# Gates and branch projections with tokens on partitions, merged rows turned by VectorE and DRAM

## The chip, the cores and the metric

The kernel runs on one core of a Trainium2 chip. A core has a matrix engine (TensorE, PE in the profile; its weight loads are PEld), a vector engine (VectorE, DVE), a scalar engine (ScalarE, ACT), a general engine (GpSimd, POOL) and a queue engine that issues transfers (SyncE, SP). They run side by side and wait for each other by semaphores. Data lies in a working memory of 128 partitions (SBUF), in the matrix engine's accumulation banks (PSUM) and in DRAM. The metric is the device time of one execution in microseconds (us). Lower is better.

## The reference

The model is an encoder of two layers on 256 tokens with 1024 channels, all in float32. The part that matters here is the token mixer of each layer:

```python
def _token_mixer(xn, w_in, w_pool, pool_scale, w_a, w_b, w_o, rel_bias):
    u, q, k, v, g_pool, g_attn = jnp.split(xn @ w_in, SPLITS, axis=-1)
    ...   # pool_out (256 x 1024) from u, attn_out (256 x 512) from q, k, v
    merged = jax.nn.sigmoid(g_pool) * (pool_out @ w_a) + jax.nn.sigmoid(g_attn) * (attn_out @ w_b)
    return merged @ w_o
```

The result is added to the residual, and a normalisation, a gated MLP with a short convolution, and another residual follow. So four products stand before the merge: the pool branch (1024 x 1024), the pool gate and the attention gate (1024 x 1024 each) and the attention branch (512 x 1024). One product stands behind it: the output projection (1024 x 1024).

## The kernel before

**Numbers in two parts.** Every float32 operand of a large product is split into a high part, rounded to the matrix engine's format (fp32r), and a low part, the rest. A product is the sum of three: high x high, high x low and low x high. ACT makes the high part of a weight piece with a copy (line 191), DVE the low part with a subtraction (line 192).

**Weights.** The class `Weights` plans all loads at the start. A load is 1 MB and goes into one of three raw buffers (`RAW`); it holds two pieces of 128 x 1024 numbers. A piece is split into one of five pairs of buffers named `wh` and `wl` (`BUFS`), up to three pieces ahead of the one in use (`LOOK`); the first four pieces of the MLP go to buffers of their own that lie idle at that time. `load` issues on SP, `_split` makes the split, `get` hands a piece out, `free` gives it back. `queue_behind` takes a few instructions and a number of pieces, whose splits are then issued behind these instructions on ACT and DVE. Each engine works its instructions off in one fixed order, which a scheduler sets when the kernel is built. The SP queue, too, is worked off in order: a transfer whose buffer is not yet free holds up those behind it.

**Products with channels on partitions.** `proj` takes a piece of 128 output channels and all 1024 input channels as the stationary side, and the tokens as the moving side. `two_sums` issues, for each of the eight input chunks, one matmul of 512 columns (the high weights with the high and the low parts of the 256 tokens, side by side) and one of 256 columns (the low weights with the high parts). That is a pair per input chunk. The two sums lie in two halves of a bank, and `add_up` (lines 567 and 568) adds them: ACT copies one, DVE adds the other.

**Products with tokens on partitions.** The value projections and the start of the MLP use `v_sum`: 128 tokens are the stationary side, and 512 output channels of the weights are the moving side. Each input chunk takes three matmuls of 512 columns. The output projection (`residual_mm`, lines 573 to 575) works in this form too, since it is added to the residual, which lies by tokens. Its first four input chunks run over both token halves and both channel halves at once (48 matmuls); the last four are held and used output by output, so that the norm of the first outputs can begin.

**The order around the change.** The pool branch (`pa`, lines 1073 to 1077) runs in eight chunks of 128 channels, with steps of the attention between them. Then come eight chunks of the pool gate (`gate`, a tanh in place of the sigmoid, with the halves folded in elsewhere), which multiply `pa`. Then, twice, four chunks of the attention gate and four of the attention branch (`b_ps`): DVE multiplies and adds, and the merged chunk `m` of 128 channels is split by ACT (line 1111) and DVE (line 1112) into the two parts `mh` and `ml`, which the output projection takes as its stationary side. Channels are on partitions throughout, as the output projection wants them.

Of the kernel before, what the change touches and what calls it, by code (L numbers as in the profile page):

```python
# [16 lines left out]
P = 128  # L17
# [77 lines left out]
class Weights:  # L95
# [8 lines left out]
    def __init__(self, tc, pool, idle):  # L104
# [5 lines left out]
        self.behind, self.n_behind = (), 0  # L110
# [35 lines left out]
    def queue_behind(self, insts, n):  # L146

        self.behind, self.n_behind = insts, self.n_split + n

    def _split(self, upto):  # L150
        nc = self.nc
        first = self.n_split
        while self.n_split < len(self.pieces):
# [7 lines left out]
            with ExitStack() as queued:  # L161
                if i < self.n_behind:
                    for inst in self.behind:
                        queued.enter_context(self.tc.issue_after(inst.ins))
# [56 lines left out]
def encoder(ctx, tc, x, w_in, w_pool, pool_scale, w_a, w_b, w_o, norm1, norm2, w_up, conv_w,  # L221
# [28 lines left out]

    for l in range(DEPTH):
# [20 lines left out]
        for c in range(4):  # L272
            W.use(cols(w_a[l], c * 256))
        for c in range(4):
            W.use(cols(w_in[l], C_GP + c * 256))
        for c in range(2):
            W.use(cols(w_in[l], C_GA + c * 512))
            W.use(cols(w_in[l], C_GA + c * 512 + 256))
            src = w_b[l][:, c * 512 : (c + 1) * 512].rearrange("(k p) c -> p k c", p=P)
            W.use(  # L280
                W.add(
                    src, (4, 512),
                    [((lambda t, j=j: t[:, :, j * 256 : (j + 1) * 256]), (4, 256)) for j in (0, 1)],
                )
            )
        for c in range(4):
            W.use(rows(w_o[l], c * 256))
        slots = (("v1",), ("ybig",), ("at2",))
# [236 lines left out]
    def columns(banks, wh, wl, k0=0):  # L525


        return [
            (
                ps,  # L530
                lambda k, c=c: wh[:, k0 + k, c * P : (c + 1) * P],
                lambda k, c=c: wl[:, k0 + k, c * P : (c + 1) * P],
            )
            for c, ps in enumerate(banks)
        ]

# [20 lines left out]
    def halves(a):  # L557

        return a.rearrange("p (t m) -> p t m", t=2)
# [89 lines left out]
    def v_sum(ps, x2, t, n, piece):  # L649
# [3 lines left out]
        for m, (part, w, j) in enumerate(passes):  # L653
            nc.tensor.matmul(  # L654
                ps, x2[:, 2 * n + j, part, t, :], w[:, j, :], start=(n + m == 0),
                stop=(n == 3 and m == 5),
            )

# [178 lines left out]
    for l in range(DEPTH):  # L837
# [235 lines left out]
        pa = big.tile([P, KD, S], F32, tag="ybig", name="pa")  # L1073
        for c in range(KD):
            add_up(pa[:, c, :], proj(po2))
            if c not in (1, 6):
                step()
# [3 lines left out]
        gates = big.tile([P, 4, S], F32, tag="gates", name="gates")  # L1081

        def gate(c):
            th = gates[:, c % 4, :]
# [181 lines left out]
```

## Time and profile before

| | |
|---|---|
| time, median of 3 runs | 874.62 us (874.56 to 874.74) |
| the profiled execution's own time | 874.7 us |
| its span, first to last instruction | 872.8 us |
| PE busy | 865.6 us (99%), 4807 matmuls |
| DVE busy | 680.1 us (78%) |
| ACT busy | 526.1 us (60%) |
| POOL busy | 31.3 us (4%) |
| read from DRAM | 159.8 MB, 184 GB/s over the span |

The profile is one execution, taken by the hardware. A group line names a source line, an engine, an operation and what it writes and reads, then a count, the busy time in us and the mean ns of one, and the idle time of the engine before these instructions with what ended it. A transfer line gives the size and the median time from its issue to its landing. The chain of work that ended last is followed back from the last instruction, at each step to what released it; an engine's share of it tells what the time is made of. The lines of `proj` and `add_up` are those of a helper, so their groups are told apart by the tiles' names: `po` is the pool branch's input, `x` the normed tokens, `at` the attention's output.

### The profile page before, as it was taken

Reading aid. Unit: us, or ns where it says so; the run is one execution under the profiler, and the core shown is the slowest. Engines: PE = TensorE matmul, PEld = TensorE weight load, DVE = VectorE, ACT = ScalarE, POOL = GpSimd, SP = SyncE. Lnnn points to the kernel's source line nnn. Section 1 sums busy time; section 2 is a strip of 40 time slices with the busy share of each in tenths; the row PEclk is TensorE's granted clock in tenths of the full one; section 3 lists DMA queues with packets and bytes.
Section 4 is the critical chain, followed back from the end, with each engine's and each line's share of the span. In section 5 each row is a group of like instructions: output and inputs, shape, how many; then the busy total and the mean of one; then the engine's idle time right before and its main releaser. Section 6 shows DMA issues by size and latency. Waiting matters only on the chain.

```text
span 872.8 us, 12725 instructions
## 1 busy us (share of the span) xinstructions
PE 865.6 (99%) x4807; PEld 756.8 (87%) x4807; DVE 680.1 (78%) x1158; ACT 526.1 (60%) x927; POOL 31.3 (4%) x98
## 2 busy tenths in 40 slices
PE   9999999999999999999999999999999999999997
PEld 8888889988888888888888889999888888888886
DVE  7998786757869978878855987776678698887874
ACT  7656554556647766666545674545666486666662
POOL 1800000000000000000000000000000000000000
PEclk9999999999999999999999999999999999999999
DMA  9676545345555475465636565453556446556531
GB/s 331 234 250 201 185 149 190 128 163 193 189 173 193 153 232 193 156 228 196 240 121 219 168 219 168 146 185 105 193 180 229 158 156 223 190 174 212 193 145 49
DMA packets 125958, 161.70 MB, mean 185 GB/s; under 512 B 3320, under 2 KB 106432, under 8 KB 125896
## 3 DMA queue, kind: packets, MB, share of 16 engines
q1 hardware_dynamic: 125736, 160.62, 54.7%
q8 instruction: 38, 0.62, 0.3%
q10 hardware_dynamic: 160, 0.27, 0.1%
q14 instruction: 24, 0.20, 0.1%
HBM read 159.80 MB, written 1.07 MB: 184 GB/s over the span
## 4 chain that ended last, share of the span: by engine, by line
PE 99%; DMA 0%; ACT 0%; POOLq 0%; issue 0%; DVE 0%; SPq 0%; POOL 0%; DVEq 0%; ACTq 0%
PE proj_ps L519 61%; PE v_ps L654 6%; PE res_ps L575 6%; PE res_ps L573 6%; PE res_ps L574 6%; PE b_ps L519 3%; PE v_ps L829 3%; PE v_ps L736 1%; PE pool_ps L519 1%; PE o_ps L1020 1%; PE s_ps L970 1%; PE pt_ps L999 1%; PE s_ps L965 1%; PE o_ps L1016 1%; PE xt_ps L457 1%; DMA raw<-in_w_in_dram 0%
## 5 line engine op out<-in xcount | busy, mean ns | idle before, releaser
L192 DVE TENSOR_TENSOR wl<-raw,wh 128x1024 fp32r<-128x1024 f32 x274 | 334.0, 1223 | 108.7 <-ACT wh L191 54.4
L191 ACT CAST wh<-raw 128x1024 fp32r<-128x1024 f32 x274 | 286.2, 1049 | 84.6 <-PE proj_ps L519 36.5
L519 PE MATMUL proj_ps<-x,wh 128*128 128x512 f32 x1408 | 335.0, 390 | 0.0
L519 PEld LDWEIGHTS proj_ps<-x,wh 128*128 128x128 f32 x1408 | 260.5, 188 | 51.7
L519 PEld LDWEIGHTS proj_ps<-x,wl 128*128 128x128 f32 x1408 | 176.7, 191 | 4.2
L519 PE MATMUL proj_ps<-x,wl 128*128 128x256 f32 x1408 | 179.8, 283 | 0.0
L573 PE MATMUL res_ps<-wh,actq 128*128 128x512 f32 (+1 forms) x184 | 70.0, 380 | 0.0
L574 PE MATMUL res_ps<-wl,actq 128*128 128x512 f32 (+1 forms) x184 | 69.9, 380 | 0.0
L575 PE MATMUL res_ps<-wh,actk 128*128 128x512 f32 (+1 forms) x184 | 69.9, 380 | 0.0
L574 PEld LDWEIGHTS res_ps<-wl,actq 128*128 128x128 f32 x184 | 34.6, 188 | 6.6
L575 PEld LDWEIGHTS res_ps<-wh,actk 128*128 128x128 f32 x184 | 34.6, 188 | 6.6
L573 PEld LDWEIGHTS res_ps<-wh,actq 128*128 128x128 f32 x184 | 34.6, 188 | 6.6
L1192 ACT ACTIVATE y<-y 128x256 f32<-128x256 f32 x44 | 18.1, 416 | 28.5 <-DVE y L1183 28.4
L519 PE MATMUL proj_ps<-po,wh 128*128 128x512 f32 x128 | 32.2, 396 | 0.0
L430 POOL TENSOR_SCALAR ss<-ss 128x1 f32<-128x1 f32 x8 | 2.0, 244 | 799.4 <-ACT junk L423 799.4
L1179 ACT ACTIVATE y<-a,prm 128x256 f32<-128x256 f32 x36 | 21.6, 600 | 14.8 <-DVE a L568 14.8
L519 PEld LDWEIGHTS proj_ps<-po,wh 128*128 128x128 f32 x128 | 23.1, 189 | 4.2
L573 PE MATMUL res_ps<-wh,m 128*128 128x512 f32 (+1 forms) x72 | 26.5, 368 | 0.0
L575 PE MATMUL res_ps<-wh,m 128*128 128x512 f32 (+1 forms) x72 | 26.3, 365 | 0.0
L574 PE MATMUL res_ps<-wl,m 128*128 128x512 f32 (+1 forms) x72 | 26.3, 365 | 0.0
L567 ACT COPY gates<-proj_ps 128x256 f32<-128x256 f32 x32 | 11.9, 373 | 23.4 <-PE proj_ps L519 23.4
L423 ACT ACTIVATE junk<-h 128x512 f32<-128x512 f32 (+1 forms) x19 | 10.5, 553 | 25.5 <-DVE h L421 25.3
(209 smaller groups left out, 1130.1 us busy)
## 6 DMA issues: line engine op xcount, KB each, us to landing
raw<-in_w_in_dram SPq DMA_DIRECT2D x58, 1024.0 KB, 5.2
raw<-in_w_up_dram SPq DMA_DIRECT2D x44, 1024.0 KB, 6.4
raw<-in_w_down_dram SPq DMA_DIRECT2D x22, 1024.0 KB, 4.9
raw<-in_w_a_dram SPq DMA_DIRECT2D x8, 1024.0 KB, 5.1
raw<-in_w_o_dram SPq DMA_DIRECT2D x8, 1024.0 KB, 4.8
raw<-in_w_b_dram SPq DMA_DIRECT2D x4, 1024.0 KB, 4.8
raw<-in_w_pool_dram SPq DMA_DIRECT2D x2, 1024.0 KB, 5.0
gain<-in_norm_dram SPq DMA_DIRECT2D x3, 512.0 KB, 4.3
```

Of the source, the lines that this page charges most:

```text
L191: lambda: nc.scalar.copy(out=h, in_=src),
L192: lambda: nc.vector.tensor_sub(out=l, in0=src, in1=h.bitcast(F32)),
L423: nc.scalar.activation(junk[:, 0 : cc.stop - cc.start], h[:, t, cc], AF.Square, scale=D**-0.5, accum_out=ss[:, n : n + 1],)
L519: nc.tensor.matmul(out, w(k), x, start=(steps is first and k == 0), stop=(steps is last and k == nk - 1), skip_group_check=turns["rest"],)
L567: nc.scalar.copy(out=out, in_=sums[1])
L573: nc.tensor.matmul(ps, ah, wh, start=first, stop=False, skip_group_check=on)
L574: nc.tensor.matmul(ps, ah, wl, start=False, stop=False, skip_group_check=on)
L575: nc.tensor.matmul(ps, al, wh, start=False, stop=last, skip_group_check=on)
L654: nc.tensor.matmul(ps, x2[:, 2 * n + j, part, t, :], w[:, j, :], start=(n + m == 0), stop=(n == 3 and m == 5),)
L829: nc.tensor.matmul(ps[t], a[:, k, t, :], w[:, j, :], start=(k + m == 0), stop=(k == KD - 1 and m == 2),)
L1179: nc.scalar.activation(y, a, AF.Identity, bias=b, scale=w1)
L1192: nc.scalar.activation(y2, y, AF.Square, scale=float(np.sqrt(0.044715)))
```

## The change

The pool branch, both gates and the attention branch are computed with tokens on partitions: `by_tokens` takes two banks, one for each 128 tokens, and runs `v_sum` over pieces of 256 input channels x 512 output channels. The weights are cut accordingly (`rows` in place of `cols`). All matmuls of these products are 512 columns wide, three per input chunk, token half and channel half. `two_sums` stays for the other products; `columns` goes.

The gates' tanh reads its bank directly, and the pool branch is copied by ACT from its bank; there are no two sums to add any more. The merged rows now have tokens on partitions, but the output projection still wants channels there. So each half of 512 channels is turned: `turn_blocks` has DVE turn it in blocks of 32 x 32 numbers, and `to_chunks` writes the turned blocks to DRAM (one transfer of 512 KB), reads them back (four transfers of 128 KB, each to 32 partitions), and splits them into `mh` and `ml` with two instructions each on ACT and DVE. This happens once per half, so twice in each layer. All five transfers go through the SP queue.

`queue_behind` can now hold several entries, each with a range of pieces. In the built kernel the splits of the fourth output-projection piece stand behind the first half's last split; the low parts of the last four stand behind the last turn; and the first four pieces of the MLP stand behind the second half's last split.

```diff
--- before.py
+++ after.py
@@ -107,7 +107,7 @@
         self.n_loaded, self.n_split, self.n_got = 0, 0, 0
         self.raw, self.split = {}, {}
         self.live = set()
-        self.behind, self.n_behind = (), 0
+        self.behind, self.later = (), []
         self.n_scaled, self.gains = 0, None
 
     def add(self, src, shape, cuts, tag=None):
@@ -143,9 +143,12 @@
             self.nc.sync.dma_start(out=t[:, c : c + step], in_=src[:, c : c + step])
             yield
 
-    def queue_behind(self, insts, n):
-
-        self.behind, self.n_behind = insts, self.n_split + n
+    def queue_behind(self, insts, n, first=0):
+
+
+        first = max(first, self.n_split)
+        self.later = self.later[-2:] + [(insts, range(first, first + n))]
+        self.behind = insts
 
     def _split(self, upto):
         nc = self.nc
@@ -159,8 +162,8 @@
                 break
             self.load(n + 1)
             with ExitStack() as queued:
-                if i < self.n_behind:
-                    for inst in self.behind:
+                for insts, some in self.later:
+                    for inst in insts if i in some else ():
                         queued.enter_context(self.tc.issue_after(inst.ins))
                 for part in self.open_next():
                     for make in part[:2]:
@@ -248,6 +251,7 @@
             tag,
         )
 
+    first_up = []
     for l in range(DEPTH):
         for g in range(NG):
             c0 = C_V + g * 512
@@ -269,22 +273,15 @@
                 pool = (pool[:1], pool[1:])
             W.use(pool[0] + cols(w_in[l], C_Q + c * 256))
             W.use(pool[1] + cols(w_in[l], C_K + c * 256))
-        for c in range(4):
-            W.use(cols(w_a[l], c * 256))
-        for c in range(4):
-            W.use(cols(w_in[l], C_GP + c * 256))
-        for c in range(2):
-            W.use(cols(w_in[l], C_GA + c * 512))
-            W.use(cols(w_in[l], C_GA + c * 512 + 256))
-            src = w_b[l][:, c * 512 : (c + 1) * 512].rearrange("(k p) c -> p k c", p=P)
-            W.use(
-                W.add(
-                    src, (4, 512),
-                    [((lambda t, j=j: t[:, :, j * 256 : (j + 1) * 256]), (4, 256)) for j in (0, 1)],
-                )
-            )
+        for w, c0 in ((w_a[l], 0), (w_in[l], C_GP)):
+            for c in (c0, c0 + 512):
+                W.use(rows(w, 0, 4, c, 512) + rows(w, 512, 4, c, 512))
+        for c in (0, 512):
+            W.use(rows(w_in[l], 0, 4, C_GA + c, 512) + rows(w_in[l], 512, 4, C_GA + c, 512))
+            W.use(rows(w_b[l], 0, 4, c, 512))
         for c in range(4):
             W.use(rows(w_o[l], c * 256))
+        first_up.append(len(W.pieces))
         slots = (("v1",), ("ybig",), ("at2",))
         for j in range(2):
             W.use(rows(w_up[l], j * 512, 4, 0, 512), slots[2 * j : 2 * j + 2])
@@ -521,18 +518,6 @@
                     stop=(steps is last and k == nk - 1), skip_group_check=turns["rest"],
                 )
         turns["rest"] = not turns["rest"]
-
-    def columns(banks, wh, wl, k0=0):
-
-
-        return [
-            (
-                ps,
-                lambda k, c=c: wh[:, k0 + k, c * P : (c + 1) * P],
-                lambda k, c=c: wl[:, k0 + k, c * P : (c + 1) * P],
-            )
-            for c, ps in enumerate(banks)
-        ]
 
     ready = []
 
@@ -646,15 +631,53 @@
     def v_tile():
         return acc.tile([P, 512], F32, tag="acc", name="v_ps")
 
-    def v_sum(ps, x2, t, n, piece):
+    def v_sum(ps, x2, t, n, piece, last=3):
+
 
         _, (wh, wl) = piece
         passes = [(0, wh, 0), (0, wl, 0), (1, wh, 0), (0, wh, 1), (0, wl, 1), (1, wh, 1)]
         for m, (part, w, j) in enumerate(passes):
             nc.tensor.matmul(
                 ps, x2[:, 2 * n + j, part, t, :], w[:, j, :], start=(n + m == 0),
-                stop=(n == 3 and m == 5),
+                stop=(n == last and m == 5),
             )
+
+    def by_tokens(x2, n, at_once=1, then=None):
+
+        ps = [mmp.tile([P, 512], F32, tag="mm", name="t_ps") for _ in range(2)]
+        for i0 in range(0, n, at_once):
+            held = [W.get() for _ in range(at_once)]
+            for t in range(2):
+                for i, piece in enumerate(held, i0):
+                    v_sum(ps[t], x2, t, i, piece, n - 1)
+            for i, _ in held:
+                W.free(i)
+            if then:
+                then()
+        return ps
+
+    def turn_blocks(y, t, rows):
+
+        return nc.vector.transpose(out=y[:, :, :, t, :].rearrange("p q c j -> p c q j"), in_=rows)
+
+    def to_chunks(y, z, x2):
+
+
+
+        d = dram.tile([P, 4, 256], F32, tag="turned", bufs=2, name="turned")
+        nc.sync.dma_start(out=d, in_=y.rearrange("p q c t j -> p q (c t j)"))
+        for q in range(4):
+            src = d[:, q].rearrange("(a i) x -> i a x", a=4)
+            nc.sync.dma_start(out=z[32 * q : 32 * q + 32].rearrange("p a c t j -> p a (c t j)"), in_=src)
+        for c in range(0, 4, 2):
+            cs = slice(c, c + 2)
+            src = z[:, :, cs].rearrange("p a c t j -> p a (c t) j")
+            hi, lo = (p[:, cs].rearrange("p c t (a j) -> p a (c t) j", a=4) for p in x2)
+            last = (
+                nc.scalar.copy(out=hi, in_=src),
+                nc.vector.tensor_sub(out=lo, in0=src, in1=hi.bitcast(F32)),
+            )
+        return last
 
     def two_parts(tag, name):
 
@@ -1070,47 +1093,52 @@
                 if m >= 3 and n % 2:
                     step()
 
-        pa = big.tile([P, KD, S], F32, tag="ybig", name="pa")
-        for c in range(KD):
-            add_up(pa[:, c, :], proj(po2))
-            if c not in (1, 6):
-                step()
+
+        pa = big.tile([P, 2, D], F32, tag="ybig", name="pa")
+        places = iter(range(KD))
+        for cc in HALVES:
+            ps = by_tokens(po2, 4, then=lambda: step() if next(places) not in (1, 6) else None)
+            for t in range(2):
+                nc.scalar.copy(out=pa[:, t, cc], in_=ps[t])
         assert not steps
 
 
-        gates = big.tile([P, 4, S], F32, tag="gates", name="gates")
-
-        def gate(c):
-            th = gates[:, c % 4, :]
-            add_up(th, proj(x2, 2))
-            nc.scalar.activation(th, th, AF.Tanh, scale=0.5)
+        def gate():
+            th = big.tile([P, 2, 512], F32, tag="gates", name="gates")
+            ps = by_tokens(x2, 4)
+            for t in range(2):
+                nc.scalar.activation(th[:, t], ps[t], AF.Tanh, scale=0.5)
             return th
 
-        for c in range(KD):
-            th = gate(c)
-            nc.vector.scalar_tensor_tensor(
-                out=pa[:, c, :], in0=th, scalar=1.0, in1=pa[:, c, :], op0=ALU.add, op1=ALU.mult
-            )
+        for cc in HALVES:
+            th = gate()
+            for t in range(2):
+                nc.vector.scalar_tensor_tensor(
+                    out=pa[:, t, cc], in0=th[:, t], scalar=1.0, in1=pa[:, t, cc],
+                    op0=ALU.add, op1=ALU.mult,
+                )
         m2 = big.tile([P, 2, KD, 2, P], F32R, tag="m2", name="m2")
         mh, ml = m2[:, 0], m2[:, 1]
-        for c4 in range(2):
-            ths = [gate(4 * c4 + j) for j in range(4)]
-            for j2 in range(2):
-                i, (wh, wl) = W.get()
-                both = [mmp.tile([P, 2, S], F32, tag="mm", name="b_ps") for _ in range(2)]
-                two_sums(at2, 4, *columns(both, wh, wl))
-                for j, ps in enumerate(both):
-                    c = 4 * c4 + 2 * j2 + j
-                    m = sm.tile([P, S], F32, tag="u", name="m")
-                    add_up(m, (ps[:, 0], ps[:, 1]))
+        z = big.tile([P, 2, 4, 4, 2, 32], F32, tag="q1", name="merged")
+        for n, cc in enumerate(HALVES):
+            th = gate()
+            ps = by_tokens(at2, 2, 2)
+            y = big.tile([P, 4, 4, 2, 32], F32, tag=("q0", "k0")[n], name="turned")
+            for t in range(2):
+                with tc.issue_after(last[1].ins) if n else ExitStack():
                     nc.vector.scalar_tensor_tensor(
-                        out=m, in0=ths[2 * j2 + j], scalar=1.0, in1=m, op0=ALU.add, op1=ALU.mult
+                        out=th[:, t], in0=th[:, t], scalar=1.0, in1=ps[t], op0=ALU.add, op1=ALU.mult
                     )
-                    nc.vector.tensor_add(out=m, in0=m, in1=pa[:, c, :])
-                    m = halves(m)
-                    nc.scalar.copy(out=mh[:, c], in_=m)
-                    nc.vector.tensor_sub(out=ml[:, c], in0=m, in1=mh[:, c].bitcast(F32))
-                W.free(i)
+                    nc.vector.tensor_add(out=th[:, t], in0=th[:, t], in1=pa[:, t, cc])
+                    turned = turn_blocks(y, t, th[:, t])
+                last = (None, turned)
+            ks = slice(4 * n, 4 * n + 4)
+            last = to_chunks(y, z[:, n], (mh[:, ks], ml[:, ks]))
+            if n == 0:
+
+                W.queue_behind(last, 5, first_up[l] - 5)
+        W.queue_behind((turned,), 4, first_up[l] - 4)
+        W.queue_behind(last, 4, first_up[l])
 
         x2 = two_parts("x", "x2")
         norm = Norm(to_channels(x2, acc, g2))
```

## The prediction, made before the changed kernel was run

> **What bounds the kernel now.** I read the chain that ended last first, from the page, to see which engine a saving has to come from.
>
> ```profile
> PE 99%; DMA 0%; ACT 0%; POOLq 0%; issue 0%; DVE 0%; SPq 0%; POOL 0%; DVEq 0%; ACTq 0%
> ```
>
> TensorE (PE) is the chain, and it waits for 1.0 us in the whole span, in two places in the opening. So every nanosecond of PE work taken away is time saved, and every wait put before PE is time added: no slack elsewhere absorbs it. Next, the same chain in order of time (start, length, what), for the pitch of PE's two kinds of work:
>
> ```profile
> 174.22 33.38 PE proj_ps L519 x192
> 207.60 5.57 PE b_ps L519 x32
> ...
> 443.83 27.23 PE v_ps L654 x120
> ```
>
> The 192 matmuls of the gates are 96 pairs of one 512-wide and one 256-wide matmul: 33.38/96 = 0.3477 us a pair. The 32 of the attention branch are 16 pairs of 0.348. The 120 of the value projection are all 512 wide: 27.23/120 = 0.2269 each. This is the form that the change goes to. Then the groups by line, for the work of VectorE (DVE) and ScalarE (ACT) between the branches and the output projection:
>
> ```profile
> L192 DVE TENSOR_TENSOR wl<-raw,wh 128x1024 fp32r<-128x1024 f32 x274 | 334.0, 1223 | 108.7 <-ACT wh L191 54.4 <-PE proj_ps L519 45.7 <-issue 6.8
> L191 ACT CAST wh<-raw 128x1024 fp32r<-128x1024 f32 x274 | 286.2, 1049 | 84.6 <-PE proj_ps L519 36.5 <-PE res_ps L575 22.6 <-DMA raw<-in_w_up_dram 7.5
> L421 DVE TENSOR_TENSOR h<-res_ps,h 128x512 f32<-128x512 f32 x12 | 8.2, 687 | 6.7 <-PE res_ps L575 6.7
> L816 ACT CAST x<-xu 128x512 fp32r<-128x512 f32 x4 | 2.4, 614 | 1.6 <-DVE xu L811 1.6
> ```
>
> A weight piece costs ACT 1.05 and DVE 1.22; a 128x512 step costs DVE 0.69 and ACT 0.61. Last, the transfers (size, median us from issue to landing) and the SP queue around the one existing trip through DRAM:
>
> ```profile
> raw<-in_w_o_dram SPq DMA_DIRECT2D x8, 1024.0 KB, 4.8
> bt<-fd SPq DMA_DIRECT2D x5, 256.0 KB, 5.7
> out_dram<-xn SPq DMA_DIRECT2D x3, 256.0 KB, 2.4
> ```
>
> ```profile
> 52.06 0.37 SPq L131 DMA_DIRECT2D raw<-in_w_pool_dram  x1
> 52.52 5.00 SPq L398 DMA_DIRECT2D bt<-fd  x5
> ```
>
> See the second: a 256 KB read issued 0.46 us behind a 1 MB load needs 5.7 us to land, although 256 KB alone are stored in 2.4. Transfers of the SP queue go in order.
>
> **What the change saves on PE.** Per layer it recasts the pool branch (64 pairs), both gates (128) and the attention branch (8 chunks of 4, 32): 224 pairs x 0.3478 = 77.9 us. In their place stand 224 x 1.5 = 336 matmuls of 512 x 0.2269 = 76.2 us. Saved: 1.7 a layer, 3.4 in all. No other PE work changes. Evacuation gets cheaper (two ACT copies of 512 in place of an ACT copy and a DVE add per 256 columns), but that lay beside PE, so it is worth nothing. The new form needs a weight piece every 12 x 0.227 = 2.72 us; ACT needs 1.05 and DVE 1.22 for it, so PE keeps being fed. The loads are cut into runs of 2 KB instead of 1 KB, the same bytes; they land in 4.8 where they are rows already (w_o) and in 5.2 where not (w_in), both far inside the 5.4 us that a load's two pieces last: nothing.
>
> **What it adds: the way from the branches to the output projection.** Before, a merged chunk of channels was cast on the spot. Now each half (512 channels) is merged by DVE (multiply, add, turn, for both token halves), written to DRAM, read back by four reads, and cast. The first half has 72 matmuls = 16.3 us of PE work over it (second gate half and branch half) and needs about 15, so I cost it at nothing; what it does is keep DVE busy until just before the second half. The second half has only the output projection's first four steps over it: 48 x 0.227 = 10.9 us. I work it out with T = the moment PE starts the output projection (229.7 in layer 0 of before), by the order in which the built kernel's instructions stand on each engine.
>
> DVE's order for the second half is: multiply of token half 0, the low part of the fourth output-projection piece, add, turn, multiply of half 1, add, turn. There are five weight buffers, so this fourth piece takes that of the first piece of the last branch weight, which PE leaves six matmuls before T: T-1.4. ACT casts it to T-0.3, DVE's low part is done at T+1.0, and five steps of 0.69 with a few hundredths between them end at T+4.6 to T+4.8. A turn is in no row; its bounds are 0.49 (L987, one input, 128x512) and two passes, 1.22. I take 0.69, the copy of the same size out of PSUM (L1155, 0.68), the nearest in shape.
>
> The write (512 KB) is issued at T+4.8. Two stores of 256 KB issued 0.4 us apart land 2.4 us after the first (864.1 to 866.5): T+7.2.
>
> Between the write and the reads stands a 1 MB load of w_up on SP. It needs a raw buffer, that is, the low parts of two more pieces, which DVE makes behind the last turn: T+4.8 + 2 x 1.22 = T+7.2. It lands 4.7 to 5.0 later (least and median of all loads): T+12.1.
>
> The four reads of 128 KB are issued behind it, from T+7.6, and go in order: the bias reads ran at some 300 GB/s behind their load, so 512 KB take 1.7 us: T+13.8. Without the load in front they would need 2.4 like the stores, or 3.1 as they are issued 0.4 apart, and land by T+10.3: this is the lower end. In all SP issues twenty transfers more (0.4 each), and the write makes it wait for the turn; behind that stand w_up loads whose pieces PE wants only after the output projection, at T+22, so this costs nothing by itself.
>
> ACT waits for all four, then casts (0.61): T+14.5. PE wants this at T+10.9: a wait of 3.6. The low part follows 0.69 later, and PE wants it two matmuls on: 0.3 more.
>
> Behind it on DVE: three low parts of w_up pieces (3.7 us) stand ahead of the first residual add, and ACT's casts for them start only after the merged ones. The second add of h, which was PE-bound at 5.6 us after PE reached its fifth step, comes some 7.5 after PE resumes; the norm's row chain takes 2.5 from there, and PE's turning of the normed rows, which had about 0.6 us to spare, waits some 0.5 (0 to 1.3).
>
> Sum per layer: 3.6 + 0.3 + 0.5 = 4.4 added, 1.7 saved, 2.7 net; two layers 5.4. The profiled execution took 874.7 (span 872.8 and 1.9 around it; the median is 874.62, the same within 0.1): **880.1**.
>
> Bounds of the added part per layer: 0.8 if the reads land by T+10.3 (0.3 for the cast, 0.3, 0.2); 3.5 if they queue, with turns of 0.49 and the norm on time; 6.3 with turns of 1.22 (1.1 more) and the norm 1.3 late (0.8 more). One thing stands apart: the reads fill 32 partitions each. [...]
>
> **Rivals.**
> (1) *The return is on time*; faster. Place: the four reads. It needs them not to queue behind the w_up load, or DVE's part to end three us earlier. For it: transfers were busy only a half of the time here (DMA share 0.49 to 0.58 around 216 to 240). Against: the load is earlier in the queue, and the bias reads. It decides where the wait per layer falls under 1.7. With 0.8 a layer: 874.7 - 3.4 + 1.6 = 872.9.
> (2) *Half on time*: the load's transfer is mostly through when the reads come, the wait is 1.3 to 2.1 a layer, some 1.7: 874.7, no change.
> (3) *The clock falls in the wait.* Mechanism: a PE that stands still loses its granted clock.
>
> ```profile
> 866.70:869.10 2.40, 0.00 (x0) 0.00 (x0) 0.91 (x2) 1.20 (x3) 0.76 (x2) 1.00 0.00 0
> 869.10:872.80 3.70, 0.00 (x0) 0.00 (x0) 0.00 (x0) 0.00 (x0) 0.00 (x0) 0.50 0.38 144
> ```
>
> These stretches (PE, weight loads, DVE, ACT, POOL, granted clock) begin after PE's last matmul at 866.6: 2.5 us later the clock is at 0.50. My wait of 3.6 is longer. Against: no wait inside the kernel shows it. Price: the opening's matmuls start at 0.8 and the clock stands at full by 5.5, so at most 4.7 us at half speed, 2.4 lost; I take 1.5 a layer, of which 0.2 hide the late norm: 874.7 + 5.4 + 2.6 = 882.7. [...]
> (4) *The first half is late too*: its reads stand behind a w_o load and land some 12 us after its branch, ACT wants them at 12.8. If they are 2 us later, DVE's second half moves with them: 874.7 + 5.4 + 2 x 1.0 = 882.1.
>
> **How the numbers follow.** Chances: forecast 0.53 (878.3 to 883.9 by its own bounds of 3.5 and 6.3), clock 0.17, first half late 0.06, half on time 0.10, on time 0.14. 0.2% (1.75 us) is about what a measurement of this kernel can tell from no change. So faster 0.14, same 0.10, slower 0.76. The range reaches from rival 1 to the upper end of the forecast, which the clock's case reaches too: 872.9 to 884.0.
>
> **What the profile after would show.** PE's stretches of 48 matmuls on t_ps at 10.9 us instead of 11.1; the transpose on DVE at some 0.69; a write landing in 2.4 and reads 5 to 6 us after their issue; one wait of 3 to 4 us on PE at L558, released by the cast of L677, and a short one at L560 by L678, per layer; a short wait before the transposes of the normed rows. I am wrong if the reads land within 3.5 us of the write, if the turn costs far from 0.69, or if the clock falls.

## The result, and the profile after

The changed kernel took 887.61 us (median of 6 runs, 883.65 to 890.09) against 874.59 for the kernel before, measured beside it. The ratio is 1.0144, with a 95% interval of 1.0121 to 1.0167: slower by 1.4%. The prediction said 880.1, within 872.9 to 884.0. The direction was right, the time lies outside the range. The profiled execution took 887.53 (span 885.7), 12.8 more than the profiled one of before (span 872.8).

In the chain that ended last, shares of the span by engine, PE has fallen from 99% to 92%, and a chain of transfers and of DVE, SP and ACT steps has come into it:

```profile
PE 92%; DMA 4%; DVE 2%; SPq 1%; ACT 1%; issue 0%; POOLq 0%; POOL 0%; ACTq 0%
```

PE's waits (who waited for whom: us in total, times, longest us). Before, there was nothing on this list beyond the opening's 1.0; behind the opening there is now one entry:

```profile
PE res_ps L558 <- ACT m L677: 10.2, 2, 5.8
```

So the output projection waits once per layer for the cast of the second half of the merged rows. The same chain in order of time, layer 0 (start, length, what), shows how the return comes about:

```profile
174.01 46.29 PE t_ps L640 x204
...
221.32 4.76 DMA merged<-turned
...
226.18 0.63 ACT m L677
226.83 0.56 DVE m L678
227.44 0.68 DVE m L678
228.13 0.60 DVE gates L1129
228.72 1.14 DVE wl L195
229.86 0.61 DVE gates L1132
230.50 0.71 DVE turned L661
...
232.54 0.72 DVE turned L661
233.28 2.96 DMA turned<-turned
...
237.57 5.41 DMA merged<-turned
243.08 0.63 ACT m L677
243.75 0.80 PE res_ps L558
244.54 0.43 PE res_ps L559
```

Read it from the top. The new products have the pitch that was forecast, 46.29/204 = 0.2269 us. The lines from 221.32 to 227.44 are the first half's return: its reads, its cast and its low parts, and DVE starts on the second half only behind them. The chain in layer 1 runs the same way. PE starts the output projection at T = 228.28. DVE merges and turns until 233.25, the write takes 2.96 to land, the fourth read 5.41, and the cast lets PE go on at 243.75. PE had been ready since 239.32: a wait of 4.43, and in layer 1 one of 5.77. And then the matmuls come 0.43 apart where 0.23 is their pitch: the clock has fallen. Stretches of 3.41 us around the two waits (busy us and number of instructions of PE, weight loads, DVE, ACT and POOL, then granted clock, DMA share and GB/s), first layer 0:

```profile
239.61:243.02 3.41, 0.00 (x0) 0.00 (x0) 0.00 (x0) 0.00 (x0) 0.00 (x0) 1.00 1.09 298
243.02:246.43 3.41, 2.68 (x6) 2.11 (x7) 2.52 (x4) 3.35 (x5) 0.00 (x0) 0.50 0.64 212
246.43:249.85 3.42, 3.42 (x9) 2.64 (x8) 2.84 (x3) 1.57 (x2) 0.00 (x0) 0.50 0.25 72
249.85:253.26 3.41, 3.41 (x16) 2.82 (x15) 1.94 (x3) 0.90 (x3) 0.37 (x1) 1.00 0.89 288
```

and layer 1:

```profile
676.51:679.93 3.42, 0.00 (x0) 0.00 (x0) 0.00 (x0) 0.00 (x0) 0.00 (x0) 1.00 1.08 300
679.93:683.34 3.41, 2.03 (x5) 1.62 (x6) 1.88 (x3) 2.70 (x4) 0.00 (x0) 0.50 0.75 257
683.34:686.75 3.41, 3.41 (x10) 2.67 (x9) 2.91 (x3) 2.22 (x3) 0.00 (x0) 0.50 0.07 23
```

In each layer the clock stands at 0.50 for 6.83 us, in which PE works for 2.68 + 3.42 = 6.1 and 2.03 + 3.41 = 5.4 us. At full clock that is half as long: 3.05 + 2.7 = 5.8 us lost. With the waits of 10.2 this makes 16.0, against a gain that the third experiment measures in its profile as 3.0 (span 869.8). 16.0 - 3.0 = 13.0; the spans differ by 12.9.

### The profile page after: what moved, and what is told of

Read it like the earlier page. It is cut to its first block, busy times and chain, and to the rows that moved or that the text cites. A ratio compares the mean times of both kernels' runs of the same rounds, so it can differ in the third digit from the quotient of the medians.

```text
span 885.7 us, 12137 instructions
## 1 busy us (share of the span) xinstructions
PE 868.5 (98%) x4583; PEld 748.1 (84%) x4583; DVE 661.9 (75%) x1070; ACT 509.3 (57%) x847; POOL 31.0 (3%) x98
## 4 chain that ended last, share of the span: by engine, by line
PE 92%; DMA 4%; DVE 2%; SPq 1%; ACT 1%; issue 0%; POOLq 0%; POOL 0%; ACTq 0%
PE proj_ps L516 45%; PE t_ps L640 14%; PE v_ps L640 6%; PE res_ps L558 6%; PE res_ps L559 6%; PE res_ps L560 6%; DMA merged<-turned 2%; PE v_ps L852 2%; PE pool_ps L516 1%; PE v_ps L759 1%; DMA turned<-turned 1%; PE pt_ps L1022 1%; PE o_ps L1043 1%; PE s_ps L993 1%; PE s_ps L988 1%; PE o_ps L1039 1%
## 5 line engine op out<-in xcount | busy, mean ns | idle before, releaser
L516 PE MATMUL proj_ps<-x,wh 128*128 128x512 f32 x1152 | 274.5, 390 | 0.0
L516 PEld LDWEIGHTS proj_ps<-x,wh 128*128 128x128 f32 x1152 | 213.1, 188 | 42.2
L516 PEld LDWEIGHTS proj_ps<-x,wl 128*128 128x128 f32 x1152 | 144.9, 191 | 3.6
L516 PE MATMUL proj_ps<-x,wl 128*128 128x256 f32 x1152 | 147.9, 283 | 0.0
L640 PE MATMUL t_ps<-wh,x 128*128 128x512 f32 x256 | 79.6, 390 | 0.0
L640 PEld LDWEIGHTS t_ps<-wh,x 128*128 128x128 f32 x256 | 48.1, 188 | 10.0
L640 PE MATMUL t_ps<-wl,x 128*128 128x512 f32 x128 | 49.8, 389 | 0.0
L640 PE MATMUL t_ps<-wh,po 128*128 128x512 f32 x128 | 42.7, 399 | 0.0
L558 PE MATMUL res_ps<-wh,m 128*128 128x512 f32 (+1 forms) x72 | 29.1, 404 | 10.2 <-ACT m L677 10.2
L1207 ACT ACTIVATE y<-a,prm 128x256 f32<-128x256 f32 x36 | 21.6, 600 | 14.7 <-DVE a L553 14.7
L640 PEld LDWEIGHTS t_ps<-wl,x 128*128 128x128 f32 x128 | 24.0, 188 | 4.9
```

The source lines that it names most:

```text
L516: nc.tensor.matmul(out, w(k), x, start=(steps is first and k == 0), stop=(steps is last and k == nk - 1), skip_group_check=turns["rest"],)
L558: nc.tensor.matmul(ps, ah, wh, start=first, stop=False, skip_group_check=on)
L640: nc.tensor.matmul(ps, x2[:, 2 * n + j, part, t, :], w[:, j, :], start=(n + m == 0), stop=(n == last and m == 5),)
L1207: nc.scalar.activation(y, a, AF.Identity, bias=b, scale=w1)
```

## The experiments

The theory after the result: the time is the saving of the new form, plus PE's wait for the second half's return, plus the clock that falls in this wait. The wait is longer than forecast because of the return's own parts (the load in front of the reads, the reads' rate, the first half ahead of it). The rivals were that the clock only accompanies something else, that the load in front is all of the wait, and that the new form itself is slower. All profiled spans below are set against the 869.8 of the kernel without the trip.

### PE kept busy over the return

```diff
+        if keep:
+            keep()
         then, half = None, None
...
+            ps = mmp.tile([P, 512], F32, tag="mm", name="idle_ps")
+            for _ in range(16):
+                nc.tensor.matmul(ps, mh[:, 0, 0, :], mh[:, 0:2], start=True, stop=True)
```

> Sixteen matmuls of 512 columns whose result nobody reads (3.6 us) are put on PE in each layer between the output projection's fourth and fifth step, where PE now stands still for 4.4 us (layer 0) and 5.8 us (layer 1). Theory (the 13 us lost are 10.2 us of waiting for the second half's return, plus some 5.8 us because the halved clock then lasts 6.8 us in each layer, less 3.4 us saved on PE): the wait is used up by the idle matmuls and is no longer, the clock stays at full, 881.8 us (881 to 883). Rival (the clock record goes with the wait but costs nothing by itself): 887.6 us. Rival (PE waits for something that comes a fixed time after it gets there, not for the return): 894 us, as the idle matmuls add 7.3 us.

It took 883.76 (881.92 to 886.86), ratio 1.0109 (1.0085 to 1.0134): by the medians faster than the changed kernel by 3.9, although PE does more (the ranges of the two overlap). PE's waits:

```profile
PE res_ps L558 <- ACT m L679: 3.5, 2, 2.1
```

The stretches of 3.41 us in layer 0 and then in layer 1 (columns as above):

```profile
240.53:243.94 3.41, 2.05 (x10) 1.36 (x8) 0.06 (x1) 0.71 (x2) 0.00 (x0) 1.00 1.10 300
243.94:247.35 3.41, 3.41 (x14) 2.50 (x15) 3.23 (x4) 3.41 (x5) 0.00 (x0) 1.00 0.36 126
...
677.44:680.85 3.41, 1.65 (x6) 1.10 (x7) 1.50 (x3) 2.32 (x4) 0.00 (x0) 1.00 0.98 301
680.85:684.26 3.41, 3.41 (x10) 2.65 (x9) 3.41 (x4) 2.60 (x3) 0.00 (x0) 0.50 0.04 6
```

In layer 0 PE stood still for 1.4 us and the clock stayed. In layer 1 the return came later, PE stood still for 2.1 us, 1.76 of them inside one stretch, and the clock fell for 3.41. So the clock's loss is of its own, and it goes when PE has work; but the sixteen matmuls did not cover the whole wait. The four runs show what this leaves to chance: the two with a mean granted clock of 0.999 and 1.000, which has no room for a fall, took 881.9 and 882.7, as expected; the two with 0.998 and 0.997 took 884.8 and 886.9.

### The reads ahead of the load

```diff
+                if self.reads is not None and self.first_late <= self.n_loaded < self.first_late + 2:
+                    queued.enter_context(self.tc.issue_after(self.reads.ins))
                 self.last = self.nc.sync.dma_start(out=t, in_=src)
...
+        W.first_late = W.pieces[first_up[l]][0] + 1
```

> One transfer changes its place: the load of the second half of the first w_up rows is issued on SP behind the second half's four reads, not between the write and them. Theory (the reads are late because they queue behind that 1 MB load): they are issued about 7.5 us after PE starts the output projection and need about 3.5 us to land instead of 6 to 7, the wait falls from 4.4 and 5.8 us to 1 to 2 us, the clock has no time to fall, and the kernel takes 874 to 877 us. Rival (the trip through DRAM is slow by itself, through the write's completion and the four narrow reads): the wait falls by under 1 us a layer and the clock still falls, 884 us or more.

880.98 (878.36 to 885.73), ratio 1.0092 (1.0061 to 1.0123). Its waits, and the return in its chain in order of time:

```profile
PE res_ps L562 <- ACT m L681: 4.3, 2, 2.2
```

```profile
232.88 2.96 DMA turned<-turned
...
237.18 3.15 DMA merged<-turned
```

The read lands 3.15 behind its issue instead of 5.41, and the waits go from 10.2 to 4.3. So the load in front is about half of the wait: in layer 0, where the last turn ended at T + 4.9 for T + 5.0, the wait fell from 4.4 to 2.1. In layer 1 it fell from 5.8 to 2.2, but there the last turn also ended at T + 4.9 instead of T + 6.0, which this edit does not touch. Of the profiled run's 6.8 us over the kernel without the trip (876.6 against 869.8), 4.3 is waiting and 1.7 a fall of the clock for 3.41 us in layer 1, behind a wait of only 2.24. This is the fastest of the four runs; the three others have a mean granted clock of 0.994 or 0.995 against its 0.997, so they spent more time at half clock.

### No trip through DRAM

```diff
-        d = dram.tile([P, 4, 256], F32, tag="turned", bufs=2, name="turned")
-        nc.sync.dma_start(out=d, in_=y.rearrange("p q c t j -> p q (c t j)"))
...
-            src = z[:, :, cs].rearrange("p a c t j -> p a (c t) j")
+            src = y[:, :, cs].rearrange("p a c t j -> p a (c t) j")
```

> The write and the reads are left out; ACT and DVE split what the turn left in place, so the merged values that the output projection gets are wrongly placed and the output is not the reference's. All else is the changed kernel. Theory (PE's part of the change is worth 3.4 us and everything lost comes from the trip): no wait of PE, 874.6 - 3.4 = 871.2 us (870.8 to 872.0). Rival (the token form of the products is itself dearer than by its pitch, through weight loads, bank changes or late weight pieces): 874.6 us or more.

871.73 (871.32 to 871.84), ratio 0.9966 (0.9953 to 0.9979). PE waits in the opening only:

```profile
PE gain_ps L345 <- PEq L1271: 0.8, 1, 0.8
```

This is the other half of the change alone. The new form saves 2.8 us by the medians (874.55 - 871.73; forecast 3.4), nothing of it is late, and its five runs lie within 0.5 us, where those of the changed kernel lie within 6.4. All the loss is in the trip.

### Reads that fill all partitions

```diff
-            src = d[:, q].rearrange("(a i) x -> i a x", a=4)
-            nc.sync.dma_start(out=z[32 * q : 32 * q + 32].rearrange("p a c t j -> p a (c t j)"), in_=src)
+            nc.sync.dma_start(out=z[:, q].rearrange("p c t j -> p (c t j)"), in_=d[:, q])
```

> The four reads of each half keep their size (128 KB) and their pieces of 1 KB, but each goes to all 128 partitions instead of 32, so the values are wrongly placed and the output is not the reference's. Theory that the reads ran at half rate because of their 32 partitions: their part of the transfer falls from 2.6 us to about 1.4, the wait falls by 1.1 to 1.2 us in each layer, 885.3 us, and 882 us if the clock then keeps up in one of the layers. Rival (their pace of some 230 GB/s is that of 1 KB pieces read back from DRAM): no change, 887.6 us.

881.58 (881.39 to 883.93), ratio 1.0087 (1.0072 to 1.0102), waits:

```profile
PE res_ps L558 <- ACT m L676: 6.5, 2, 3.4
```

While the reads' data flow, in the changed kernel (32 partitions each; last columns granted clock, DMA share, GB/s):

```profile
240.50:242.50 2.00, 0.00 (x0) 0.00 (x0) 0.00 (x0) 0.00 (x0) 0.00 (x0) 1.00 1.12 256
```

and in this kernel (128 partitions):

```profile
240.00:241.50 1.50, 0.00 (x0) 0.00 (x0) 0.00 (x0) 0.00 (x0) 0.00 (x0) 1.00 1.07 374
```

The transfer engines are as busy in both, with pieces of 1 KB in both, but move 256 GB/s in the one stretch and 374 in the other. The median read lands after 4.4 instead of 6.1. The wait falls from 4.4 to 3.4 in layer 0 and from 5.8 to 3.0 in layer 1. Only the first is mostly the reads' rate: the last turn ended 0.2 us earlier there than in the changed kernel, and 2.1 us earlier in layer 1, because the first half came back sooner. The clock now falls for one stretch of 3.41 in each layer and not for two: 6.5 + 2 x 1.7 = 9.9, and the span is 879.7 - 869.8 = 9.9 longer. The time is near the 882 of the expectation by luck: that needed the clock to hold through one of the layers, and it fell in both. That reads of 32 partitions go at half the rate was the author's assumption, and no run shows it: these stretches lose a third (256 of 374). Nor does a run isolate what the partitions cost: the four narrow reads go to four different groups of 32 partitions, some pieces of the next load lie in both stretches, and the edit also changes the order in which the rows are read.

### Reads first, and PE kept busy

The edits of the first two experiments together, with ten matmuls in place of sixteen.

> As the run with the reads ahead of the load, and PE also runs ten unread 512-wide matmuls (10 x 0.227 = 2.27 us a layer) in the time of the two waits of 2.1 to 2.2 us that were left there; the output is the same. Theory (the waits and the clock are all there is): the waits go to under 0.2, the clock never falls, and the time is 874.6 - 3.4 + 2 x 2.27 = 875.7, from run to run within 1 us. Rival (something behind the return is late as well, DVE's low parts or the norm): PE waits elsewhere by 0.5 to 1.3 a layer, 877 to 878.5.

880.72 (880.43 to 883.44), ratio 1.0066 (1.0049 to 1.0083): neither expectation. The waits of the profiled run:

```profile
PE res_ps L562 <- ACT m L683: 2.3, 2, 1.8
```

The matmuls took their 2.27 us a layer, but the second half came back later than in the kernel that it builds on: its casts start 13.2 and 14.4 us behind T, there 12.5 and 12.6. What is late there is the first half. In both kernels its reads still stand behind a w_o load, its own casts start 1.5 and 1.2 us ahead of T instead of 2.2, and DVE's work on the second half is queued behind its low parts. So the cover was eaten up, and in the profiled run (883.44, span 881.6) the clock also fell twice for 3.41 us, in the opening at 6.99 and in layer 1. In the three other runs, at 880.4 to 880.9, the mean granted clock (0.999) leaves no room for a fall; where they lose what lies above the expected 875.7 is open, since the slowest run alone has a trace.

### Wide reads that reach the right places, in front of the load

```diff
-        for q in range(4):
-            src = d[:, q].rearrange("(a i) x -> i a x", a=4)
-            W.reads = nc.sync.dma_start(out=z[32 * q : 32 * q + 32].rearrange("p a c t j -> p a (c t j)"), in_=src)
+        for a in range(4):
+            src = d[32 * a : 32 * a + 32].rearrange("i q x -> q i x")
+            W.reads = nc.sync.dma_start(out=z[:, a].rearrange("p c t j -> p (c t j)"), in_=src)
```

> As the run with the reads ahead of the load, but each of the four reads takes a block of 32 tokens, so that it fills all 128 partitions with 1 KB pieces, and not 32 partitions; the same bytes come to the same places. Theory (a read that fills 32 partitions goes at half the rate, and the rest of the way is as counted): the reads land 2.1 to 2.4 us behind their issue instead of 2.9 to 3.2, the wait per layer falls from 2.15 to 1.0 to 1.4; without a fall of the clock 874.6 - 3.4 + 2.4 = 873.6, with one fall of 3.41 us (1.7) 875.3. Rival (the rate belongs to this trip through DRAM and not to the partitions): the wait stays at 2.1, and so does the time, 878 to 882.

896.98 (895.18 to 898.15), ratio 1.0243 (1.0227 to 1.026): the slowest of all, and foreseen by neither expectation. The waits, and the transfers while the reads flow (last columns as above):

```profile
PE res_ps L562 <- ACT m L681: 17.7, 4, 7.4
```

```profile
241.50:244.00 2.50, 0.00 (x0) 0.00 (x0) 0.00 (x0) 0.00 (x0) 0.00 (x0) 1.00 0.27 92
```

Two of the four waits are for the first half, at T. The reads show a quarter of the transfer engines' time (0.27) and 92 GB/s, a quarter of the 374 with pieces of the same size. The source pattern now begins with a dimension of 4 where the others begin with 32 or 128. That this is what costs the rate is the author's reading; no run changes it alone. The theory's half rate for 32 partitions this run does not show either. In layer 0 the last read landed 6.38 behind its issue, against 3.15 with the narrow reads ahead of the load: this way of filling all partitions cost more than it gave.

### The same with a shorter chain on DVE

The edit is the one shown below for narrow reads, on the kernel just told.

> As the run with the reads first and wide, and the low part of the fourth output-projection piece (1.2 us on DVE) moved from between the second half's multiply and add to behind its last turn, with the load that follows it kept behind the reads. Theory: the return comes 1.2 us earlier, so the wait of 1.0 to 1.4 per layer is gone or under 0.3, the clock stands, and the time is 874.6 - 3.4 + 0 to 0.6 = 871.2 to 871.8, as without the trip. Rival (the fourth piece, now later, makes PE wait at the fourth step, or the loads that stand behind the reads are late): 872.5 to 875.

893.08 (892.48 to 893.21), ratio 1.0199 (1.0185 to 1.0213). It falls with its parent, whose reads it keeps. It is 3.9 faster than the parent, with waits of 12.8 instead of 17.7.

### PE turns the second half

```diff
+                    turned = nc.vector.tensor_add(out=th[:, t], in0=th[:, t], in1=pa[:, t, cc])
+                    if n == 0:
+                        turned = turn_blocks(y, t, th[:, t])
...
+                for k in range(4):
+                    nc.tensor.transpose(pt[:, k, :], th[:, t, k * P : (k + 1) * P], ident)
...
+        for k, _ in enumerate(residual_mm(lambda k: (mh[:, k], ml[:, k]), KD, norm.add, fill=begin_mlp)):
+            if k == 2:
+                turn_second()
```

> The second half of the merged rows takes no way through DRAM: PE turns it by eight 128x128 transposes per layer behind the third step of the output projection, and ACT and DVE take the two parts out of PSUM; the first half is as in the changed kernel. Theory (only the second return costs): PE does 8 x 0.11 = 0.9 us more a layer and waits for nothing, the clock stands, and the time is 874.6 - 3.4 + 1.8 = 873.0, under the kernel before by 0.2%. Rival (the first half's return is late too, or DVE is): a wait of 1 to 3 us per layer at the fifth step, with a fall of the clock, 876 or more.

873.74 (872.69 to 875.21, 12 runs) against 874.61, ratio 0.9986 (0.9977 to 0.9995). Its chain by engine is PE alone again:

```profile
PE 99%; ACT 0%; POOLq 0%; issue 0%; POOL 0%; ACTq 0%
```

There is no wait but the opening's, the clock does not fall before PE's last matmul, and the span is 870.9, which is 1.1 over the kernel without any trip. This profile is of the fastest of the twelve runs; by the medians the distance is 2.0 (873.74 against 871.73; forecast 1.8 for sixteen transposes). It is the only complete kernel here that is faster than the one before, by 0.14% (0.05 to 0.23). It also shows that one half's trip through DRAM, with 16 us of PE work over it, makes PE wait for nothing when no second trip is queued behind it.

### Reads first, and a shorter chain on DVE

```diff
-                if self.reads is not None and self.first_late <= self.n_loaded < self.first_late + 2:
+                if self.reads is not None and self.first_late <= self.n_loaded < self.first_late + 3:
...
-        W.first_late = W.pieces[first_up[l]][0] + 1
-        W.queue_behind((turned,), 4, first_up[l] - 4)
+        W.first_late = W.pieces[first_up[l]][0]
+        W.queue_behind((turned,), 5, first_up[l] - 5)
```

> As the run with the reads ahead of the load (by 32 partitions, as in the changed kernel), and the low part of the fourth output-projection piece (1.2 us on DVE) moved from between the second half's multiply and add to behind its last turn, with the w_up load that follows it kept behind the reads as well. Theory: everything from the add on is 1.2 us earlier, so PE's wait falls from 2.1 to 2.2 to 0.9 to 1.1 per layer. If the clock stands through a wait of that length: 874.6 - 3.4 + 2.0 = 873.2. Rival (any wait of PE at this place can bring a fall of 3.41 us, 1.7 us lost): 874.9 to 876.6. Rival (the fourth piece, now later, stops PE at the output projection's fourth step): a wait at that step, 874 to 877.

881.41 (877.99 to 882.35), ratio 1.007 (1.0051 to 1.0089): no gain over the run with the reads first. PE's waits, and from DVE's timeline (start, length, what, the idle time before it and its releaser) the step behind the second of them:

```profile
PE res_ps L562 <- ACT m L681: 3.9, 2, 2.4
PE xt_ps L458 <- DVE xn L449: 2.5, 1, 2.5
```

```profile
246.42 1.23 DVE L199 TENSOR_TENSOR v<-raw,v 128x1024 fp32r<-128x1024 f32 x1 [4.18 <-ACT v L198]
```

Two things ate the 1.2 us. The first half's casts came 0.9 to 1.1 us later than in the run with the reads first, and with them the second half. And the w_up load that was moved behind the reads is now late itself: ACT and DVE wait for its pieces (4.18 us on DVE), these stand ahead of the residual adds, and the norm makes PE wait for 2.5. This is the late norm of the prediction. The clock fell once in each layer, at 253.77 behind the norm's wait and at 677.03 behind the wait of 2.4 for the second half.

### Both halves' reads first

As the last, and one line more:

```diff
                 W.queue_behind(last, 5, first_up[l] - 5)
+                W.first_late = W.pieces[first_up[l] - 4][0]
```

> As the run with the reads first and the low part moved, and the first half's reads too are issued ahead of the w_o load that stood before them. Theory (the second half's multiply waits on DVE for the first half's low parts, so the first half's return sets it as well): the first half lands 2 to 2.5 us earlier, the second half's multiply starts 0.8 to 0.9 us earlier, and PE's wait goes from 0.9 to 1.1 to under 0.3; the clock stands; 874.6 - 3.4 + 0 to 0.6 = 871.2 to 871.8, faster than before by 0.3 to 0.4%. Rival (the first half is hidden, as the prediction had it): as the run without this edit, 873.2 or more. Rival (the w_o load, now later, is late for its pieces): a wait at the seventh step, 873 to 876.

875.29 (873.68 to 877.81, 11 runs), ratio 1.0008 (0.9997 to 1.0018): 6.1 us for one line. The waits:

```profile
PE xt_ps L458 <- DVE xn L449: 0.8, 2, 0.7
PE res_ps L562 <- ACT m L681: 0.3, 1, 0.3
```

The first half's casts start 3.8 us ahead of T, DVE ends its last turn at T + 2.9 instead of T + 4.8 and T + 5.0 in the kernel without this line, and the wait for the second half is all but gone, as expected; in the profiled run (874.55) the clock stays. So the first half's return does set the second's. What that run has over the 871.2 to 871.8 of the theory is the late norm (0.8), the wait of 0.3, and matmuls behind the return that start 0.1 to 0.5 late each. The ten other runs, up to 877.81, have no trace.

### What the clock goes by

All the falls behind the opening fit one pattern. In the changed kernel the clock fell at 243.02, 679.93 and, after PE's last matmul, 884.73 us: 128 and 60 times 3.413 us apart. The trace's clock changes lie on a fixed grid of this step, which does not follow the kernel: counted from the span's start, the fall at 243.02 lies 0.67 behind a multiple of the step, the fall at 869.10 in the kernel before 2.11. I laid this grid over the profiled execution of each kernel here, and took PE's idle time in each window that lies between 11 us and PE's last matmul, where it was over 0.35 us:

| PE idle in a window of 3.41 us, at full clock | windows | clock at 0.50 in the next |
|---|---|---|
| 0.36 to 1.46 | 14 | 0 |
| 1.60 and 1.61 | 2 | 1 |
| 1.70 to 3.41 | 15 | 15 |

At half clock, six windows with 0.73 to 3.41 us idle all kept it for another 3.41, and windows without idle time ended it. So in these profiles the clock falls when PE is idle for about half of a window, not only for a whole one: with the wide reads first and the shorter chain on DVE, PE was busy for 1.81 of the window from 668.18 on, and the clock was at 0.50 in the next. A wait of 3.4 us holds 1.7 in one window wherever the grid lies, and 1.7 or more cost a fall in every case here; a wait between 1.6 and 3.4 should cost one or not by where the grid lies, which is worked out from the table. The opening, where PE runs a few small matmuls, does not fit: in the profiled run of the kernel with the reads first and PE kept busy, PE was idle for only 1.22 of the window from 3.57 on, and the clock fell at 6.99. Why is not shown.

## Why the prediction was wrong, point by point

- **The saving on PE** (3.4): 2.8 by the medians without the trip, 3.0 in the profiles. The pitch of 0.2269 was exact. Cheaper evacuation, the loads' new cut and the weight pieces cost nothing, as said: no wait in that run. From T in layer 0 to T in layer 1 the profiles differ by 1.4 where 1.7 was forecast; of this, 0.16 is in the attention's 24 transposes (`pt_ps`) among the new products, which take 2.53 us for 2.38. The rest is open.
- **The second half's way** from T was forecast in its order and nearly in its times up to the reads, in layer 0: the last turn ended at T + 5.0 (T + 4.8, which is luck, as the point on the first half shows; a turn takes 0.71, taken as 0.69), the load ahead was issued at T + 7.2 (T + 7.2), the reads from T + 8.0 (T + 7.6). The write's landing was mis-sized, 2.96 for 2.4.
- **"512 KB take 1.7 us"** is the first term that was mis-sized. The reads landed at T + 14.7, not T + 13.8. With wide reads the wait in layer 0 is 1.0 shorter, 0.2 of it from an earlier last turn, so most of these 0.9 us go with the narrow reads.
- **"The first half costs nothing"** failed in both layers. It cost no wait by its own cast, but DVE's second half is queued behind its low parts. The last turn ended 7.07 and 7.08 us behind the start of the first half's casts (T - 2.1 and T - 1.1), and by 7.07 to 7.08 in the nine other layers with this order of DVE's work where those casts started between T - 2.3 and T - 0.7. In the one where they started earlier, T - 3.3 in layer 1 of the wide reads, the last turn ended at T + 3.9. So in this range each microsecond by which the first half comes later puts the last turn off by one. In layer 0 this gave T + 5.0, close to the forecast T + 4.8, which had the cast of the fourth output-projection piece as the limit: the number was met by luck. In layer 1 it gave T + 6.0, and the wait was 5.77. Rival 4 had this mechanism, at 1.0 a layer; against the forecast it came to 0.2 and 1.2. The run with both reads first shows it.
- **The wait** of 3.6 a layer so became 4.4 and 5.8. The low part's 0.3 did not show in this profile, nor did the late norm's 0.5: PE ran at half clock then, and probably had no need of them sooner. The norm's does show where the clock stays, 0.8 in two layers with both reads first.
- **The clock** is the step that decided the miss. The sum took a wait of 3.6 and put the loss by the clock at nothing, an estimate that no run bears out; as a rival it had a chance of 0.17 and a price of 1.5 a layer. By the table a wait of 3.4 us or more costs a fall in any position, and the fall held for two windows: 2.9 a layer. Rival 3 was the case that came, too cheap and too unlikely. The evidence lay in the trace of before, at the end of the kernel: 0.50 only 2.5 us after the last matmul, less than a window of 3.41.

By its own chain with the measured sizes: 874.7 - 3.0 + 10.2 + 5.8 = 887.7, against 887.53. Term by term from the forecast: 5.8 more for the clock, 3.0 more for the two waits (10.2 for 7.2), 0.4 less saved, and 1.6 less for the low parts and the norm. Without the clock's 5.8 it would be 881.9, inside the range.

What stays open: why the first half's return moves by some 2.5 us between kernels that do not touch it (its casts start between 0.8 and 3.3 us ahead of T in the complete kernels with its narrow reads behind the w_o load and in the one with wide reads), and how much of the changed kernel's spread of 6.4 us is the grid's place under the two waits. That the spread comes from both is only argued.

## What to carry to other kernels

A wait of PE, which here otherwise never rests, cost more than its length: wherever 1.70 us or more of idle time lay in one clock window of 3.41 behind the opening, the clock fell (15 of 15), and each half-clock window that PE worked through cost another 1.7. So cover such a wait with work that is needed anyway or do not make it. A trip through DRAM was free here only behind enough work, 16 us of it over the first half's in the run where PE turns the second, and its parts have to be counted one by one: here 3.0 us for a 512 KB write, 2.9 for the reads, and whatever large load stands ahead of them in the same queue. Of two trips, ask what of the second is ordered behind the end of the first. Moving a transfer past another in a queue can move the wait on to the other one's user, as with the w_up load moved behind the reads (4.18 us on DVE), so follow that one as well.

## What the runs showed of the hardware

- In these twelve profiles the granted clock changes on a fixed grid of 3.413 us. Behind the opening it fell after every window with 1.70 us or more of idle PE time (15) and after none with 1.46 or less (14), and it stayed down for one window more in all six cases where the next had 0.73 us or more.
- Reads of 1 KB pieces from DRAM flowed at 256 GB/s with 32 partitions to a read (changed kernel, 240.50 to 242.50) and at 374 with 128 (wide reads, 240.00 to 241.50); the same pieces with a source pattern that begins with a dimension of 4 at 92 (first and wide, 241.50 to 244.00).
- VectorE's turning of 128x512 float32 in blocks takes 0.71 us, about as much as its copy of that size out of PSUM (0.68).
- A 512 KB write to DRAM lands 2.96 us after its issue in layer 0 of the changed kernel, with a 256 KB store at 2.4 in the kernel before.
